# Mixer output of a hybrid decoder layer: four plain column blocks become two column pairs with partly Strassen products

## The chip, the cores and the metric

One core of one Trainium2 chip runs the whole layer in one launch. The metric is the device time of that launch in microseconds (us). TensorE is called PE, VectorE DVE, ScalarE ACT, GpSimd POOL; SP is the engine whose queue issues the weight loads. All data are float32.

## The reference

One decoder layer works on 256 tokens of width 2048. The part that matters here is the mixer's end and what follows it:

```
merged = sigmoid(gate_conv) * (y_conv @ Wa) + sigmoid(gate_hgrn) * (y_hgrn @ Wb)
x = layer_norm(ALPHA * x + merged @ mix_w_out[i], ln_g[i, 1], ln_b[i, 1])
x = layer_norm(ALPHA * x + 0.5 * swiglu(x, ffn2_w_in[i], ffn2_w_out[i]), ln_g[i, 2], ln_b[i, 2])
```

`merged` is 256 x 2048 and `mix_w_out` 2048 x 2048. The LayerNorm needs a whole row of 2048 before it can normalise any of it.

## The kernel before, in words

**Tiles.** The 256 tokens are two token tiles, t0 and t1. A k-tile is 128 rows of a weight; 2048 rows are sixteen k-tiles. A column block is 512 columns. One weight element is two k-tiles by 512 columns (128 x 1024 in SBUF, 512 KB). The tokens stand still in PE (transposed, 128 x 128) and the weight streams through.

**Three passes.** Each float32 factor is split into a high and a low part in the type fp32r: for a weight, ACT casts `raw` to `wh` (L1090) and DVE subtracts to get `wl` (L1101); for tokens, `halves` does the same (L299, L300). `passes` issues three matmuls of 512 columns per k-tile and token tile: L1160 (high, high), L1161 (`wl`), L1162 (token low). So a plain element that serves both token tiles costs PE 2 x 2 x 3 = 12 matmuls.

**The weight line.** `plan` lists all elements in the order of use. `feed` keeps the line going: a load by SP into `raw` (four buffers), a cast on ACT, a split on DVE, then PE. The pairs `wh`/`wl` come from a ring of six (`NMAIN`, called main); elements of a `Unit` may also take pairs of the stage's own ring, whose size stands in `EXTRA` ("merge": 2). A pair is free again when PE has used the element for both token tiles.

**Unit and Quad.** A `Unit` (`run_unit`) is one column block; it goes through blocks of elements, t0 first and then t1 within a block. A `Quad` (`run_quad`) is a pair of column blocks, where some k-tiles are done as Strassen products (in Winograd's form): k-tiles 0 to 7 are two steps of a 2 x 2 problem (tokens t0/t1, low and high k-tiles, left and right columns), and each step takes seven products instead of eight. A product is an element that serves one product alone: 6 matmuls on PE, one cast, one split. Four of the seven (`t1` to `t4`) need the sum of two weight buffers first, a DVE add (L1069). The eight weight buffers of a step sit in rings of their own, `raw11` (two buffers), `raw12`, `raw21`, `raw22` (one each), and a ring's next load waits until the buffer is done with. Names in `ORDER`: `11.0` is product 11 of step 0, `t3.1` is sum product 3 of step 1, `a0` and `u0` are plain elements for the left and the right block. Quad elements use the main ring only. The token operand needs four sums `s1` to `s4`, which DVE makes.

**The stages around the change.** In the stage "merge", `gate_units(c)` runs for c = 0 to 3: a Quad for the two gates, then two Units of 8 k-tiles for the two branches (L922 to L924). It leaves `merged` in the tiles `m`. When the last gate Quad is done, `to_stat` transposes `m` on PE and splits it into the operand `ms` (L904, L905, L910, L917).

Then come four Units, one for each column block of the mixer's output (L931 to L942). `epi_m` adds the result to `ALPHA * x` (L935) and takes the statistics (`ln_stat`, L425). The last block is cut into k-tiles 0 to 3 and then 4 to 15 (`LATE`): in that second part t0 runs through all of its twelve k-tiles before t1 starts. With t0's row complete, `layer_norm` runs for t0: `bn_aggr` (L448), the root (ACT, L434), four normalisations (L491); then, for each 512 columns, a transposition on PE (L286), scale and shift on ACT (L485) and the split (L299, L300) that makes the next stage's token operand `xh`/`xl`. The next stage is "lead2", the first column block of the second FFN.

All engines work their instructions off in the order in which Tile's scheduler has put them, which it does once, when the program is built.

Of the kernel before, what the change touches and what calls it, by code (L numbers as in the profile page):

```python
# [17 lines left out]
P = 128  # L18
D = 2048
S = 256  # L20
NT = 2
# [10 lines left out]
HIGH = {"11": 2, "12": 1, "21": 1, "22": 1}  # L32
EXTRA = {"lead1": 3, "ffn1": 0, "tail1": 4, "hgrn": 0, "merge": 2, "lead2": 3, "ffn2": 0, "tail2": 4, "ple": 1}
ALPHA = 2.0 ** 0.25
# [32 lines left out]
class Quad:  # L67
# [24 lines left out]
    }  # L92

    def __init__(self, stat, w, cols, width, after, form):
        self.stat, self.w, self.cols, self.width, self.after = stat, w, cols, width, after
        short = form == "short"
        self.shorted = not short
        order = self.ORDER[form].split()
        second = (("p3", 0), ("r", 1)) if form[:4] == "gate" else (("p3", "d"), ("p5", 1))
        made = {}  # L100
# [41 lines left out]
def hybrid_layer(ctx: ExitStack, tc: tile.TileContext, x, p, ln_g, ln_b, ffn1_w_in, ffn1_w_out, mix_w_in,  # L142
# [146 lines left out]
    def halves(stat, t, g, src, nb, tag, into=None):  # L289

        if into:
            h, l = into
        else:
            where, bufs = (region["pool"], 7) if tag == "s" else (op, 8)
# [5 lines left out]
        nc.vector.tensor_tensor(out=lf, in0=src, in1=hf.bitcast(F32), op=ALU.subtract)  # L300
        stat.parts[t, g] = (h, l)
# [120 lines left out]
    def ln_stat(t, c):  # L422
        if c == 0:
            stats[t] = st.tile([P, 4, 6], F32, tag="bn", name="bn", bufs=2)
        nc.vector.bn_stats(stats[t][:, c, :], xt[t][:, c * CC : (c + 1) * CC])  # L425
# [19 lines left out]
    def moments(t, scale):  # L445

        mv = st.tile([P, 2], F32, tag="mv", name="mv", bufs=2)
        nc.vector.bn_aggr(mv, stats[t])  # L448
        return mv[:, 0:1], rsqrt_of(mv[:, 1:2], 1, 1.0, LN_EPS / scale ** 2)
# [413 lines left out]
    def gate_units(c):  # L863
# [33 lines left out]
        def fifth(ps):  # L897
            both(made["conv", 1], made["conv", 1], ps["p4"], ALU.add)
            for key in (("conv", 1), ("hgrn", 0), ("hgrn", 1)):
                sigmoid(made[key])  # L900
            if c == 3:
                share_banks({"a": 4, "t": 4})
                load_stored()
                for i in range(4):  # L904
                    defer(2 + 3 * i, lambda t=i % 2, cc=i // 2: to_stat(ms, t, cc, mc[t, cc], 4, "x"))  # L905

# [5 lines left out]
        def epi_h(t, acc):  # L912
            m = mc[t, c] = made["conv", t] if c == 3 else rtile([P, CC], tag=f"m{t}{c}", name="m")
# [11 lines left out]

    mc = {}
    units.append(("merge", drain))
    for c in range(4):
        gate_units(c)

    for c in range(4):  # L931
        def epi_m(t, acc, c=c):
            settle(c)
            xc = xt[t][:, c * CC : (c + 1) * CC]
            nc.vector.scalar_tensor_tensor(out=xc, in0=xc, scalar=ALPHA, in1=acc, op0=ALU.mult, op1=ALU.add)  # L935
            ln_stat(t, c)
            if c == 3:
                layer_norm(t, 1, 1.0, x2)

        if c == 3:  # L940
            units.append(("merge", lambda: open_high("lead2")))
        units.append(Unit(ms, mix_w_out[0], 0, 16, c * CC, CC, epi_m, split=LATE if c == 3 else SPLIT))  # L942

# [238 lines left out]
    def run_quad(u, gi):  # L1182
        left = {}
        for el in u.els:
            for bank, _, ks in el["use"]:
                left[bank] = left.get(bank, 0) + len(ks)
        ps = {}
        for el in u.els:
            for i, (bank, t, ks) in enumerate(el["use"]):
                tick()  # L1190
                first = bank not in ps
                if first:
                    ps[bank] = ps["p1"] if bank == "r" else ptile("a", bank)
                for a, k in enumerate(ks):
                    left[bank] -= 1
                    passes(ps[bank], u.stat, t, k, gi, a if len(ks) > 1 else i, first and a == 0, left[bank] == 0)
            consumed(gi)
            while u.after and all(b in left and not left[b] for b in u.after[0][0]):
                _, fn, read = u.after.popleft()
                fn(ps)  # L1200
                for b in read:
                    used(ps[b])
            gi += 1
        return gi

# [44 lines left out]
```

## Time and profile before

| | |
|---|---|
| median of 3 runs | 2207.2 us (2206.49 to 2207.89) |
| the profiled execution | 2205.99 us, its span 2204.3 us |
| PE busy | 2183.2 us, 99% |
| DVE busy | 1805.5 us, 82% |
| ACT busy | 1171.4 us, 53% |
| gates and branches (stage "merge") | about 1060 to 1308 us |
| mixer's output, four Units | about 1308 to 1397 us |
| lead2 from | about 1397 us |

A time in a row of the timeline is counted from the start of the span. In the timeline a row gives start, duration, engine, line, operation and, in square brackets, how long the engine had been idle before it and who released it. A row with x3 is three instructions, merged. In a row of the windows each engine has its busy time and, in brackets, its number of instructions; PEclk is the granted clock of PE as a share.

### The profile page before, as it was taken

What the parts mean: (1) busy time and instruction counts of PE and PEld (TensorE: products, weight loads), DVE (VectorE), ACT (ScalarE), POOL (GpSimd) and SP (SyncE); (2) the same over time, 40 slices, a digit from 0 to 9 for tenths busy, and PEclk for the clock granted to TensorE, in tenths of its full rate; (3) what the DMA queues carried; (4) which work ended last, traced back from release to release, by engine and by line L of the source; (5) the groups of instructions that cost most, each with busy time, mean ns of one, the idle gap of its engine ahead of it and who ended that gap; (6) DMA issues with size and microseconds to landing.
All of it is one profiled execution on the core that took longest, in us unless ns stands there. A gap on an engine that the chain in (4) does not pass through costs nothing.

```text
span 2204.3 us, 27128 instructions
## 1 busy us (share of the span) xinstructions
PE 2183.2 (99%) x10043; PEld 1818.4 (82%) x10043; DVE 1805.5 (82%) x2046; ACT 1171.4 (53%) x1397; POOL 18.7 (1%) x48
## 2 busy tenths in 40 slices
PE   9999999999999999999999999999999999999997
PEld 7988888888887888888888888798888888888886
DVE  6799998999886677658898885679999999998667
ACT  5555555555565534534564553645555555555473
POOL 1000000000000000000000000000000000000000
PEclk9999999999999999999999999999999999999999
DMA  7666666666663665554666576466666666665564
GB/s 254 217 191 211 206 202 189 194 202 212 203 196 124 192 212 179 188 184 149 225 207 191 186 234 223 152 214 197 195 202 187 208 210 201 201 210 180 182 218 150
DMA packets 227129, 434.20 MB, mean 197 GB/s; under 512 B 14508, under 2 KB 23220, under 8 KB 226996
## 3 DMA queue, kind: packets, MB, share of 16 engines
q1 hardware_dynamic: 225716, 428.27, 61.3%
q0 software_dynamic: 1280, 4.20, 0.5%
q8 instruction: 78, 1.28, 0.2%
q14 instruction: 55, 0.45, 0.1%
HBM read 428.22 MB, written 4.19 MB: 196 GB/s over the span
## 4 chain that ended last, share of the span: by engine, by line
PE 92%; DVE 3%; DMA 2%; ACT 1%; issue 1%; DVEq 0%; SPq 0%; ACTq 0%
PE bank L1161 30%; PE bank L1162 30%; PE bank L1160 30%; DVE wl L1101 2%; PE bank L286 2%; PE bank L705 1%; DMA raw<-in_ffn_w_in_dram 1%; DMA raw<-in_ffn_w_out_dram 1%; ACT wh L1090 1%; DVE raw L1069 0%; DVE x L505 0%; DMA raw<-in_ple_w_gate_dram 0%; DVE x L506 0%; ACT y L485 0%; PE bank L675 0%
## 5 line engine op out<-in xcount | busy, mean ns | idle before, releaser
L1090 ACT CAST wh<-raw 128x1024 fp32r<-128x1024 f32 (+1 forms) x968 | 969.0, 1031 | 801.7 <-PE bank L1162 363.9
L1101 DVE TENSOR_TENSOR wl<-raw,wh 128x1024 fp32r<-128x1024 f32 (+1 forms) x968 | 1135.5, 1201 | 259.4 <-ACT wh L1090 246.4
L1162 PE MATMUL bank<-wh,xl 128*128 128x512 f32 (+1 forms) x1672 | 645.0, 387 | 2.6 <-DVE xl L300 2.5
L1161 PE MATMUL bank<-wl,xh 128*128 128x512 f32 (+1 forms) x1672 | 644.8, 387 | 0.3 <-DVE wl L1101 0.3
L1160 PE MATMUL bank<-wh,xh 128*128 128x512 f32 (+1 forms) x1672 | 636.7, 388 | 0.4 <-ACT wh L1090 0.2
L1162 PEld LDWEIGHTS bank<-wh,xl 128*128 128x128 f32 x1672 | 314.2, 188 | 65.0 <-DVE xl L300 5.2
L1160 PEld LDWEIGHTS bank<-wh,xh 128*128 128x128 f32 x1672 | 314.2, 188 | 60.9 <-ACT xh L299 0.7
L1161 PEld LDWEIGHTS bank<-wl,xh 128*128 128x128 f32 x1672 | 314.5, 188 | 60.0 <-DVE wl L1101 0.8
L1161 PE MATMUL bank<-wl,gh 128*128 128x512 f32 x896 | 349.2, 391 | 1.1 <-DVE wl L1101 1.1
L1162 PE MATMUL bank<-wh,gl 128*128 128x512 f32 x896 | 348.5, 390 | 0.0
L1160 PE MATMUL bank<-wh,gh 128*128 128x512 f32 x896 | 346.3, 393 | 0.1
L1069 DVE TENSOR_TENSOR raw<-raw,raw 128x1024 f32<-128x1024 f32 x208 | 245.5, 1181 | 13.6 <-DMA raw<-in_ffn_w_in_dram 7.2
L1161 PEld LDWEIGHTS bank<-wl,gh 128*128 128x128 f32 x896 | 168.3, 188 | 37.1 <-DVE wl L1101 3.1
L1160 PEld LDWEIGHTS bank<-wh,gh 128*128 128x128 f32 x896 | 168.2, 188 | 34.8 <-ACT gh L299 0.5
L1162 PEld LDWEIGHTS bank<-wh,gl 128*128 128x128 f32 x896 | 168.3, 188 | 34.7
L1161 PE MATMUL bank<-wl,sh 128*128 128x512 f32 x464 | 181.6, 391 | 0.0
L1162 PE MATMUL bank<-wh,sl 128*128 128x512 f32 x464 | 180.6, 389 | 0.0
L1160 PE MATMUL bank<-wh,sh 128*128 128x512 f32 x464 | 177.1, 389 | 0.0
L1160 PEld LDWEIGHTS bank<-wh,sh 128*128 128x128 f32 x464 | 87.1, 188 | 18.3
L1162 PEld LDWEIGHTS bank<-wh,sl 128*128 128x128 f32 x464 | 87.1, 188 | 17.8
L1161 PEld LDWEIGHTS bank<-wl,sh 128*128 128x128 f32 x464 | 87.1, 188 | 17.7
L299 ACT CAST gh<-bank 128x512 fp32r<-128x512 f32 (+2 forms) x54 | 30.6, 569 | 72.2 <-PE bank L286 71.6
(179 smaller groups left out, 1045.3 us busy)
## 6 DMA issues: line engine op xcount, KB each, us to landing
raw<-in_ffn_w_in_dram SPq DMA_DIRECT2D x288, 512.0 KB, 4.3
raw<-in_mix_w_in_dram SPq DMA_DIRECT2D x176, 512.0 KB, 4.6
raw<-in_ffn_w_out_dram SPq DMA_DIRECT2D x168, 512.0 KB, 4.8
raw<-in_ffn_w_in_dram SPq DMA_DIRECT2D x64, 256.0 KB, 3.0
raw<-in_mix_w_out_dram SPq DMA_DIRECT2D x32, 512.0 KB, 5.5
raw<-in_ple_w_gate_dram SPq DMA_DIRECT2D x32, 512.0 KB, 5.2
raw<-in_ffn_w_in_dram SPq DMA_DIRECT2D x32, 384.0 KB, 3.9
raw<-in_branch_w_conv_dram SPq DMA_DIRECT2D x16, 512.0 KB, 5.1
```

Source lines behind the costliest of these rows:

```text
L286: state["turned"] = nc.tensor.transpose(tp[:, i * P : (i + 1) * P], src[:, i * P : (i + 1) * P], ident).ins
L299: state["half"] = nc.scalar.copy(hf, src).ins
L705: nc.tensor.matmul(gp[:, (h * 2 + t) * 64 : (h * 2 + t + 1) * 64], kd[:, h, t * P : (t + 1) * P], qd[:, h, t, :], start=True, stop=True)
L1069: nc.vector.tensor_tensor(out=out, in0=a, in1=b, op=ALU.add)
L1090: nc.scalar.copy(h[:, :n, :w], raw[:, :n, :w])
L1101: state["split"] = nc.vector.tensor_tensor(out=l[:, :n, :w], in0=raw[:, :n, :w], in1=h[:, :n, :w].bitcast(F32), op=ALU.subtract).ins
L1160: nc.tensor.matmul(acc, sh, wh[:, a, :n], start=first, stop=False)
L1161: nc.tensor.matmul(acc, sh, wl[:, a, :n], start=False, stop=False)
L1162: nc.tensor.matmul(acc, sl, wh[:, a, :n], start=False, stop=last)
```

## The change

The four Units become two Quads, `mix_units(0)` and `mix_units(2)`, each with k-tiles 0 to 7 as Strassen products and 8 to 15 plain.

- A Quad has 14 products of 6 matmuls and 8 plain elements of 12: 180 matmuls for a pair, where two Units have 192. It has 22 elements (22 casts, 22 splits) where two Units have 16, and 8 weight adds.
- The token sums: `low_part` transposes `m` of the first two blocks soon after it is made, splits it (tag `m`), keeps a copy `mT`, and after the fourth makes the four sums; `fifth` of the last gate splits them.
- The results of the seven products are combined on DVE (`first`, `second`, `third`, `done`): twelve operations of 512 columns and four statistics for a pair, where two Units have four and four.
- The order of the last Quad, "mixend", has its last six plain elements in a tied group: `visit` runs all six for t0 and then all six for t1.
- The stage's own pairs `EXTRA["merge"]` go from 2 to 0.

```diff
+        "mix": "11.0 11.1 t1.0 a3 22.0 u3 t3.0 a0 t2.0 u0 21.0 t4.0 a1 t1.1 u1 22.1 t3.1 a2 t2.1 u2 21.1 t4.1",
+        "mixend": "11.0 11.1 t1.0 a3 22.0 t3.0 u3 t2.0 21.0 t4.0 t1.1 22.1 t3.1 t2.1 21.1 t4.1 [ a0 u0 a1 u1 a2 u2 ]",
...
-            if c == 3:
+            if c < 2:
+                defer(2, lambda: low_part(t, m))
+            elif c == 3:
                 defer(5 - t, lambda: to_stat(ms, t, 3, m, 4, "g"))
+        def low_part(t, m):
+            tp = transposed(m, 4)
+            halves(ms, t, c, tp, 4, "m")
+            mT[t, c] = rtile([P, CC], tag=f"mT{t}{c}", name="mT")
+            nc.scalar.copy(mT[t, c], tp)
+            if t + c == 2:
+                x11, x12, x21, x22 = mT[0, 0], mT[0, 1], mT[1, 0], mT[1, 1]
+                both(x22, x21, x22, ALU.subtract)
+                both(x21, x11, x21, ALU.subtract)
+                both(x11, x22, x11, ALU.subtract)
+                both(x12, x12, x11, ALU.add)
...
-        def epi_m(t, acc, c=c):
-            nc.vector.scalar_tensor_tensor(out=xc, in0=xc, scalar=ALPHA, in1=acc, op0=ALU.mult, op1=ALU.add)
-            ln_stat(t, c)
-            if c == 3:
-                layer_norm(t, 1, 1.0, x2)
-        units.append(Unit(ms, mix_w_out[0], 0, 16, c * CC, CC, epi_m, split=LATE if c == 3 else SPLIT))
+        def first(ps):
+            made["e"] = st.tile([P, CC], F32, tag="h", name="e", bufs=3)
+            nc.scalar.copy(made["e"], ps["p1"])
+            scaled(cols(0, 0), made["e"])
+        def second(ps):
+            for t in range(NT):
+                scaled(cols(t, 1), ps["p5"])
+        def third(ps):
+            e = made["e"]
+            both(e, e, ps["p6"], ALU.add)
+            both(cols(0, 1), cols(0, 1), e, ALU.subtract)
+            both(e, e, ps["p7"], ALU.add)
+            both(cols(1, 1), cols(1, 1), e, ALU.subtract)
+            scaled(cols(1, 0), e)
+        def done(t, n, bank):
+            def fn(ps):
+                both(cols(t, n), cols(t, n), ps[bank], ALU.add)
+                ln_stat(t, c + n)
+                if last and n:
+                    ...
+                    layer_norm(t, 1, 1.0, x2)
+    mix_units(0, False)
+    mix_units(2, True)
...
+        for group in u.groups:
+            for turn in range(2):
+                for n in group:
+                    if turn < len(u.els[n]["use"]):
+                        visit(u, n, turn, gi, ps, left)
```

The scheduler puts the instructions into their final order, so the order is shown at two places.

DVE before, in the middle of the mixer's output: four splits, then one result and its statistics for a column block (`wl` is a split, L935 the result, BN_STATS the statistics).

```order
L1101 TENSOR_TENSOR wl_10762<-raw_10689,wh_10761 128x1024
L1101 TENSOR_TENSOR wl_10775<-raw_10701,wh_10774 128x1024
L1101 TENSOR_TENSOR wl_10787<-raw_10713,wh_10786 128x1024
L1101 TENSOR_TENSOR wl_10799<-raw_10726,wh_10798 128x1024
L935 SCALAR_TENSOR_TENSOR x0_10359<-x0_10359,bank2_83 128x512
L425 BN_STATS bn_10677<-x0_10359 128x6
```

DVE now, where the first pair ends and the second begins: the first row is the split of `t4.1` of the first pair, the second that of `11.0` of the second pair; L1131 is a weight add, L957 a step that combines the first pair's results; `raw11_10831` is the weight buffer of the second pair's `11.1`.

```order
L1163 TENSOR_TENSOR wl_10828<-raw11_10300,wh_10827 128x1024
L1163 TENSOR_TENSOR wl_10840<-raw11_10682,wh_10839 128x1024
L1131 TENSOR_TENSOR raw11_10682<-raw11_10682,raw12_10753 128x1024
L957 TENSOR_TENSOR e_10613<-e_10613,bank6_87 128x512
L1131 TENSOR_TENSOR raw12_10753<-raw12_10753,raw22_10756 128x1024
L957 TENSOR_TENSOR x0_10397<-x0_10397,e_10613 128x512
L1163 TENSOR_TENSOR wl_10857<-raw11_10831,wh_10856 128x1024
L957 TENSOR_TENSOR e_10613<-e_10613,bank4_85 128x512
L1163 TENSOR_TENSOR wl_10867<-raw11_10682,wh_10866 128x1024
L957 TENSOR_TENSOR x0_10397<-x0_10397,bank2_83 128x512
L1163 TENSOR_TENSOR wl_10892<-raw_10695,wh_10891 128x1024
L957 TENSOR_TENSOR x0_10397<-x0_10397,bank7_88 128x512
```

Between two splits there now stand weight adds and the first pair's sums. From the split of `11.0` to the split of `t4.1` of the second pair, DVE has 15 splits, 8 adds and 18 operations of 512 columns in its order.

PE before, from t0's last matmul of the mixer's output (first row) to the first transposition of the normalised x (L286). Of the 24 matmuls between the two, all of them t1's (bank7), the first two and the last one are shown.

```order
L1162 MATMUL bank2_83<-wh_11021,gl_10567 128x512
L1160 MATMUL bank7_88<-wh_10935,xh_10485 128x512
L1161 MATMUL bank7_88<-wl_10936,xh_10485 128x512
...
L1162 MATMUL bank7_88<-wh_10997,gl_10508 128x512
L286 MATMUL bank4_85<-ident_89,x0_10359 128x128 x4
```

PE now, the same place: `wh_11127` is element `u2`, whose use with `gl_10583` in the third row is t0's last matmul; the fourth row is t1's (`gl_10632`), and L293 is the transposition.

```order
L1224 MATMUL bank4_85<-wh_11115,gl_10583 128x512
...
L1223 MATMUL bank3_84<-wl_11128,gh_10582 128x512
L1224 MATMUL bank3_84<-wh_11127,gl_10583 128x512
L1224 MATMUL bank1_82<-wh_11098,gl_10632 128x512
L293 MATMUL bank0_81<-ident_89,x0_10397 128x128 x4
L1222 MATMUL bank2_83<-wh_11115,gh_10631 128x512
L1223 MATMUL bank2_83<-wl_11116,gh_10631 128x512
```

The scheduler has put most of t1's matmuls of the tied group ahead of t0's last one: 1 of t1's matmuls is left between t0's last and the first transposition, and 12 more stand after that transposition. Before, it was 24 and 12. After those 12, both programs have the remaining transpositions and two matmuls of lead2 before the first one that reads `xl`.

More of the change, by code (lines that the diff above doesn't have):

```diff
@@ L97, in __init__ @@
         self.shorted = not short
-        order = self.ORDER[form].split()
-        second = (("p3", 0), ("r", 1)) if form[:4] == "gate" else (("p3", "d"), ("p5", 1))
+        text = self.ORDER[form]
+        order = text.replace("[", "").replace("]", "").split()
+        free, _, tied = text.partition("[")
+        n = len(free.split())
+        self.groups = [[i] for i in range(n)] + ([list(range(n, len(order)))] if tied else [])
+        second = (("p3", "d"), ("p5", 1)) if form in ("short", "long") else (("p3", 0), ("r", 1))
         made = {}
@@ L293, in halves @@
         else:
-            where, bufs = (region["pool"], 7) if tag == "s" else (op, 8)
+            where, bufs = {"s": (region["pool"], 7), "m": (region["pool"], 4)}.get(tag, (op, 8))
             h = where.tile([P, 4, P], F32R, tag=tag + "h", name=tag + "h", bufs=bufs)
@@ L1187, in run_quad, with visit @@
         ps = {}
[L1188 to L1204, printed above, removed]
+        for group in u.groups:
[3 more added lines that the diff above has]
+                        visit(u, n, turn, gi, ps, left)
+        return gi + len(u.els)
+    def visit(u, n, turn, gi, ps, left):
+        use = u.els[n]["use"]
+        bank, t, ks = use[turn]
+        tick()
+        first = bank not in ps
+        if first:
+            ps[bank] = ps["p1"] if bank == "r" else ptile("a", bank)
+        for a, k in enumerate(ks):
+            left[bank] -= 1
+            passes(ps[bank], u.stat, t, k, gi + n, a if len(ks) > 1 else turn, first and a == 0, left[bank] == 0)
+        if turn == len(use) - 1:
+            consumed(gi + n)
+        while u.after and all(b in left and not left[b] for b in u.after[0][0]):
+            _, fn, read = u.after.popleft()
+            fn(ps)
+            for b in read:
+                used(ps[b])
     gi = 0
```

40 lines of the change are left out of this document (27 added, 13 removed).

## The prediction

> **What bounds the kernel now.** The page first:
>
> ```profile
> PE 2183.2 (99%) x10043; PEld 1818.4 (82%) x10043; DVE 1805.5 (82%) x2046; ACT 1171.4 (53%) x1397; POOL 18.7 (1%) x48
> PE 92%; DVE 3%; DMA 2%; ACT 1%; issue 1%; DVEq 0%; SPq 0%; ACTq 0%
> ```
>
> The second line is the chain that ended last: PE bounds the kernel, so a matmul taken away is worth its full time as long as nothing else becomes late in that stage. DVE is next, with 82% on average. Its room differs by stage, so I read the windows: the last gate Quad first, then two stretches of the mixer's output (PE, PEld, DVE, ACT, POOL busy, clock, DMA share, GB/s).
>
> ```profile
> 1242.40:1283.30 40.90, 40.90 (x182) 33.78 (x181) 34.53 (x33) 23.01 (x25) 2.73 (x6) 1.00 0.48 148
> ```
>
> ```profile
> 1340.00:1360.00 20.00, 20.00 (x90) 16.57 (x89) 10.96 (x11) 7.10 (x7) 0.00 (x0) 1.00 0.65 210
> 1398.00:1400.05 2.05, 0.18 (x1) 0.00 (x0) 2.05 (x4) 0.83 (x1) 0.00 (x0) 1.00 0.97 347
> 1401.60:1405.00 3.40, 3.40 (x9) 2.31 (x8) 2.35 (x5) 3.40 (x8) 0.00 (x0) 0.50 0.81 259
> ```
>
> A gate Quad keeps DVE busy for 34.5 of 40.9 us with hardly anything but its weights (33 instructions, of which 30 are splits and adds); its sums fall due in the two branch Units behind it. The four plain Units use half of DVE. At the end of the mixer's output PE stands still for 1.9 us, and 1.5 us later its clock is halved for 3.4 us: the only such place in the kernel.
>
> The unit prices come from DVE's timeline: starts of neighbouring rows give what one instruction really takes from the queue.
>
> ```profile
> 1198.95 5.76 DVE L1101 TENSOR_TENSOR wl<-raw,wh 128x1024 fp32r<-128x1024 f32 x5
> 1204.63 1.22 DVE L1069 TENSOR_TENSOR raw<-raw,raw 128x1024 f32<-128x1024 f32 x1
> 1205.76 3.53 DVE L1101 TENSOR_TENSOR wl<-raw,wh 128x1024 fp32r<-128x1024 f32 x3
> ...
> 1301.34 0.68 DVE L867 TENSOR_TENSOR sig<-sig,bank 128x512 f32<-128x512 f32 x1
> 1301.94 1.22 DVE L1101 TENSOR_TENSOR wl<-raw,wh 128x1024 fp32r<-128x1024 f32 x1
> ...
> 1325.20 0.69 DVE L935 SCALAR_TENSOR_TENSOR x<-x,bank 128x512 f32<-128x512 f32 x1 [3.13 <-PE bank L1162]
> ...
> 1346.96 0.69 DVE L935 SCALAR_TENSOR_TENSOR x<-x,bank 128x512 f32<-128x512 f32 x1 [3.13 <-PE bank L1162]
> ```
>
> Five splits in 5.68 us and an add in 1.13: 1.14 us for either. An operation of 512 columns: 0.60. The last two rows are t0's results of two blocks, one Unit of 96 matmuls apart: 21.76 / 96 = 0.2267 us per matmul, so 2.72 us for a plain element and 1.36 for a product.
>
> **The change part by part.**
>
> *Matmuls.* 2 x 12 = 24 fewer: 24 x 0.2267 = **5.4 us** saved, if PE stays fed.
>
> *The gates.* Of `low_part`, the four transpositions and splits replace those of the first two blocks; new are four sums, four splits of them (8 x 0.60 = 4.8 us of DVE) and four copies on ACT. The stretch 1242 to 1283 has 6 us of DVE idle, each gate has another 21.8 us (96 matmuls) of branches behind it, and the additions spread over three gates: nothing, or up to 4.8 us if DVE were never idle there. The two missing spare pairs served branch Units alone, where PE takes 2.72 us per element and DVE 1.14: nothing.
>
> *The first pair.* DVE comes to it after the branches, with time to fill the six pairs. 30 x 1.14 + 16 x 0.60 = 43.8 us of DVE stand against 180 x 0.2267 = 40.8 us of PE, and its last sums slip into the second pair. No loss here.
>
> *The second pair.* It follows without a branch between, and starts with the first pair's sums in DVE's queue. How far can DVE be ahead? The six pairs set that, as ACT's row shows for a cast held up by PE, not by weights; and two rows give the landing time of a weight (median of this stage, then the spread before it).
>
> ```profile
> 1338.80 1.05 ACT L1090 CAST wh<-raw 128x1024 fp32r<-128x1024 f32 x1 [0.31 <-PE bank L1162]
> ```
>
> ```profile
> raw<-in_mix_w_out_dram SPq DMA_DIRECT2D x27, 512.0 KB, 5.5
> ```
>
> ```profile
> DMA to landing us min/median/max: 3.6/4.9/10.1
> ```
>
> `11.0` can be cast only when `t3.1`, six elements earlier, is used up; then PE still has `a2 t2.1 u2 21.1 t4.1`, 2 x 2.72 + 3 x 1.36 = 9.5 us. Less the cast (1.05) and the split (1.14), DVE's lead is 7.3 us at most. From there to the split of `t4.1` of this pair DVE has 15 splits, 8 adds and 18 small operations: 23 x 1.14 + 18 x 0.60 = 37.0 us. Besides, `11.1` needs the buffer that the split just ahead of `11.0`'s has freed: load 5.5 and cast 1.05, less 1.14 for the split between, makes 5.4 us, in which DVE has two adds and two sums (3.5): 1.9 us of waiting. Together 38.9 us. PE needs for the same 15 elements 13 x 1.36 + 2 x 2.72 = 23.1 us. PE idle: 38.9 - 7.3 - 23.1 = **8.5 us**. Behind it come six plain elements, where DVE gets ahead again, so nothing is added, but nothing is won back either. Ends: without the wait for the load and with a lead of 9.5 us, 4.4 us; with the longest landing, 10.1 us, 13.1. I take the median's value.
>
> *The end.* DVE's rows and PE's rows around the LayerNorm:
>
> ```profile
> 1387.76 0.69 DVE L935 SCALAR_TENSOR_TENSOR x<-x,bank 128x512 f32<-128x512 f32 x1 [7.21 <-PE bank L1162]
> ...
> 1392.37 1.92 DVE L491 TENSOR_SCALAR x<-x,mv,r 128x512 f32<-128x512 f32 x4
> 1394.20 4.63 DVE L1101 TENSOR_TENSOR wl<-raw,wh 128x1024 fp32r<-128x1024 f32 x4
> 1398.74 0.68 DVE L935 SCALAR_TENSOR_TENSOR x<-x,bank 128x512 f32<-128x512 f32 x1
> 1399.33 0.69 DVE L300 TENSOR_TENSOR xl<-yT,xh 128x512 fp32r<-128x512 f32 x1
> ```
>
> ```profile
> 1387.33 0.39 PE L1162 MATMUL bank<-wh,gl 128*128 128x512 f32 x1
> ...
> 1393.00 0.62 PE L286 MATMUL bank<-ident,x 128*128 128x128 f32 x4
> ...
> 1400.08 0.50 PE L1162 MATMUL bank<-wh,xl 128*128 128x512 f32 x1 [1.89 <-DVE xl L300]
> ```
>
> From t0's last matmul (1387.33) to the first transposition it is 5.7 us, filled before with 24 of t1's matmuls; from there to `xl`, another 7.1 us, with 12 more and the two of lead2. DVE's chain is the same now: sum, statistics, root, four normalisations, four splits, `xl`. But only 1 matmul of t1 is left for the first stretch. The 23 others have run earlier, ahead of t0's end, and hide nothing: 23 x 0.2267 = **5.2 us** of PE idle. Ends: 4.0, if a part of the chain is shorter because the left block's sum is done ahead of the right one's; 5.9, if that sum (0.60) is late as well.
>
> *Behind the restart.* t1 now has two sums and two statistics in DVE's queue ahead of the next `xl`, not one of each: 2 x 0.60 = **1.2 us**, since PE waits for these `xl`. The halved clock stays one period, as before. Ends: a loss of nothing, or of 1.2 and two more halved periods of 3.4 us, in each of which PE does half: 4.6.
>
> The trace has the clock halved after a stop of 1.9 us. The Trainium skill, TensorE: Matmul & The Clock Gate, section "Why this matters for your kernels", asks for no PE idle gaps above about 3 us between bursts of matmuls. The trace disagrees on the size: 1.89 us were enough here. By the page, the 5.2 us at the end alone would count, and the sum would stay as it is; by the trace, the stops within the second pair may count too, which is the third rival.
>
> *Sum.* - 5.4 + 8.5 + 5.2 + 1.2 = + 9.5 us. The profiled execution took 2205.99 us (span 2204.3 and 1.7 around it); it would take 2215.5. The median of the three runs lies 1.2 above it: **2216.7 us**.
>
> **The rivals.**
>
> *DVE keeps up.* If the lead is larger than I think or the sums fit into gaps, the second pair costs nothing: - 5.4 + 5.2 + 1.2 = + 1.0, 2208.2 us. For it speaks that in the last gate Quad DVE was busy for most of the time (34.5 of 40.9 us) and PE never stopped. Against it: that Quad had no sums of another one in its way. It decides at 38.9 us of DVE against 30.4 of lead and PE. Chance 0.16.
>
> *The cover is not needed.* As before, and DVE, now ahead, has t0's statistics almost done when t0 ends, so that the end costs what it cost before: - 5.4, 2201.8 us. This is the forecast's other side: faster. It decides at the 5.7 us between t0's last matmul and the transposition; those are a chain that starts with t0's last sum, which speaks against it. Chance 0.07.
>
> *The clock.* Each stop of 1.9 us or more is followed by a halved period, in the second pair and again after the restart: two periods more than before, 2 x 1.7 = 3.4 us: 2220.1 us. For it: the one case in the trace. Against it: PE waits for DVE in that stretch anyway, so a slow PE costs only what is left. Chance 0.15.
>
> **How the numbers follow.** The forecast has 0.62, the three rivals 0.16, 0.07 and 0.15. A measurement of this kernel can tell about 0.2% from no change, 4.4 us. The forecast's own ends, with the second pair at 4.4 and the end at 4.0, make - 5.4 + 4.4 + 4.0 + 0 = + 3.0 (2210.2); with the second pair at 11, between the median's and the longest landing, 5.9 and 1.2 make + 12.7 (2219.9), and with the clock's 3.4 it is 2223.3. I take 2207.5 to 2222: it holds the first rival and most of the third, and leaves out the second and the far ends. Faster by over 0.2% is the second rival alone, 0.07. Within 0.2% lie the first rival and the low end of the forecast, 0.16 + 0.05 = 0.21. Slower: 0.72.
>
> **What would show it.** Right: the timeline shows PE idle, released by the split (L1163), in the second half of the mixer's output, 6 to 11 us in all and most of it ahead of products of the second pair, with DVE at 95% and more from about the start of that pair; one stop of about 5 us right ahead of the transposition of x (L293), released by the normalisation; PE without stops in the gates. Wrong in its largest term: PE without waits for the split there; then the time lies near 2208. Wrong in the second: the transposition follows t0's last matmul with no stop. If PE stops in the gates, I have missed the cost of the earlier sums or of the missing pairs.

## The result, and the profile after

| | before | after |
|---|---|---|
| median of 4 runs | 2206.84 us (2206.26 to 2207.89) | 2221.72 us (2220.3 to 2223.46) |
| the profiled execution | 2205.99 us, span 2204.3 | 2223.46 us, span 2221.8 |

The ratio is 1.0068, with a 95% interval of 1.0056 to 1.008: slower by 14.9 us. The forecast was 2216.7 us, range 2207.5 to 2222.0. The direction held and the size was short by 5 us; the median lies just inside the range's upper end, by 0.3 us, and two of the four runs lie above it.

The page of after, the same two lines: 24 matmuls fewer, 52 instructions more on DVE and 22 more on ACT, and in the chain less PE, more of everything that PE waits for.

```profile
PE 2186.9 (98%) x10019; PEld 1816.2 (82%) x10019; DVE 1852.1 (83%) x2098; ACT 1189.7 (54%) x1419; POOL 18.6 (1%) x48
PE 90%; DVE 4%; DMA 3%; ACT 2%; issue 1%; DVEq 0%; SPq 0%; ACTq 0%
```

What PE waited for in after from 1340 to 1430 us (who waits, for whom, us in total, times, the longest). Before had one such row there, 1.9 us for `xl`.

```profile
PE bank L293 <- DVE x L498: 3.7, 1, 3.7
PE bank L1222 <- ACT wh L1152: 3.7, 5, 1.6
PE bank L1223 <- DVE wl L1163: 3.4, 2, 2.8
PE bank L1224 <- DVE xl L307: 1.8, 2, 1.3
PE bank L1222 <- ACT xh L306: 1.0, 1, 1.0
```

From the top: the stop at the LayerNorm; weights of the second pair, and one of lead2; splits of the second pair; token operands behind the restart (the last two). The casts in the second row are in the pair only the messenger: there each cast that PE waits for had itself waited for a DVE add.

The windows of after (PE, PEld, DVE, ACT, POOL, clock, DMA share, GB/s): the second pair, the LayerNorm, the restart, and what follows it.

```profile
1351.80:1385.90 34.10, 28.59 (x104) 20.77 (x103) 33.95 (x39) 15.60 (x17) 0.00 (x0) 0.90 0.25 77
1360.45:1367.25 6.80, 5.98 (x14) 4.72 (x15) 6.80 (x9) 1.12 (x2) 0.00 (x0) 0.50 0.75 231
1399.20:1403.30 4.10, 0.36 (x3) 0.03 (x1) 3.36 (x11) 2.53 (x3) 0.00 (x0) 1.00 0.00 0
1412.00:1419.00 7.00, 4.11 (x16) 2.45 (x14) 6.18 (x11) 6.74 (x13) 0.00 (x0) 0.96 0.80 245
1418.50:1425.20 6.70, 6.00 (x14) 4.75 (x15) 4.20 (x9) 2.55 (x4) 0.00 (x0) 0.50 0.69 231
```

In the pair DVE is busy for 33.95 of 34.10 us and PE for 28.6. The clock is halved twice for 6.8 us, in the pair and behind the restart; before it was once, for 3.4. (In both kernels it is halved once more at the very end, from 2193.5 us before and from 2213.8 after, where PE has no more work.)

To see where the time came from I set the same matmul of both executions side by side (counted from the start up to the end of the gates, and behind the pairs back from the end, so that the 24 missing ones drop out) and read how far after lags at six places, from the start of the stage "merge" on. The differences of neighbouring places are the cost of a stretch, in us, net of what before loses there; what the matmuls save is added back in the pairs.

| kernel | gates | pairs, to t0's end | t0's end to restart | restart to lead2's steady part | the rest |
|---|---|---|---|---|---|
| forecast | 0 | 8.5 | 5.2 | 1.2 | 0 |
| after | 1.1 | 10.9 | 3.3 | 6.6 | 1.2 |
| first pair only | 0.3 | 0.0 | -0.6 | 1.3 | 0.6 |
| second pair only | 0.3 | 2.1 | 4.2 | 0.1 | 0.0 |
| second pair only, t1 held | 0.3 | 4.6 | 0.0 | 1.8 | 0.8 |
| both, adds on POOL | 0.3 | 21.9 | 3.5 | -0.2 | 1.3 |
| both, t1 held | 0.3 | 11.8 | 0.0 | 1.4 | 1.7 |
| both, t1 held, first sums left out | 0.3 | 8.9 | 0.0 | 1.4 | 2.1 |
| both, t1 held, 11.1 late | 1.8 | 12.0 | 0.0 | 1.0 | 1.4 |
| both, t1 held, spread | 0.3 | 6.6 | 6.7 | 3.7 | 0.3 |
| both, t1 held, spread, casts behind | 0.3 | 5.2 | 2.8 | 4.7 | 1.5 |
| both, casts behind | 0.3 | 10.0 | 3.3 | 1.9 | 1.4 |
| first pair only, casts behind | 0.3 | 0.0 | -0.6 | 0.0 | 1.2 |
| first pair only, splits ahead | 0.3 | 0.0 | 4.7 | 3.8 | 0.7 |

The matmuls save 5.4 with both pairs and 2.7 with one. The table is of one profiled execution each, and ahead of the gates these differ from before by -0.8 to 1.5 us, which it leaves out; that of after is the slowest of its four, 1.7 us above their median. The ratios below are to the kernel before, run beside it on the same chip, and us from ratios are the ratio's excess times 2207.

**The second pair on DVE.** DVE's rows in after: the split of `11.0` is the last of the three in the first row (it ends at 1344.99), then come the split of `11.1` and that of `t4.1`. ACT's row holds the casts of the first pair's `t4.1` and of `11.0`, and PE's row is its first matmul of the second pair.

```profile
1341.35 3.64 DVE L1163 TENSOR_TENSOR wl<-raw,wh 128x1024 fp32r<-128x1024 f32 x3
...
1350.72 1.23 DVE L1163 TENSOR_TENSOR wl<-raw,wh 128x1024 fp32r<-128x1024 f32 x1 [2.13 <-ACT wh L1152]
...
1383.42 1.22 DVE L1163 TENSOR_TENSOR wl<-raw,wh 128x1024 fp32r<-128x1024 f32 x1
```

```profile
1341.55 2.00 ACT L1152 CAST wh<-raw 128x1024 fp32r<-128x1024 f32 x2 [2.11 <-DVE raw L1131]
```

```profile
1350.38 0.39 PE L1222 MATMUL bank<-wh,mh 128*128 128x512 f32 x1
```

From the end of the split of `11.0` to that of `t4.1` (1384.64) DVE took 39.6 us, and its lead over PE at the start, from the end of the split of `11.0` to its first use, was 1350.38 - 1344.99 = 5.4. With the prediction's 23.1 us of PE that makes 39.6 - 5.4 - 23.1 = 11.1 us lost; PE in fact took 10.9 us more for the 108 matmuls of the products, `a3` and `u3` than at full speed. The same sum fits the other kernels with both pairs: 9.8 against 9.6 with t1 held, 10.2 against 9.9 with the casts behind, 6.5 against 6.3 with the first sums left out, 9.8 against 9.5 with 11.1 late.

### The profile page after: what moved, and what is told of

The parts are those of the page before. It is cut to its first block, busy times and chain, and to the rows that moved or that the text cites. A ratio compares the mean times of both kernels' runs of the same rounds, so it can differ in the third digit from the quotient of the medians.

```text
span 2221.8 us, 27163 instructions
## 1 busy us (share of the span) xinstructions
PE 2186.9 (98%) x10019; PEld 1816.2 (82%) x10019; DVE 1852.1 (83%) x2098; ACT 1189.7 (54%) x1419; POOL 18.6 (1%) x48
## 3 DMA queue, kind: packets, MB, share of 16 engines
q8 instruction: 78, 1.28, 0.2%
## 4 chain that ended last, share of the span: by engine, by line
PE 90%; DVE 4%; DMA 3%; ACT 2%; issue 1%; DVEq 0%; SPq 0%; ACTq 0%
PE bank L1223 29%; PE bank L1222 29%; PE bank L1224 29%; DVE wl L1163 2%; PE bank L293 2%; DMA raw<-in_ffn_w_in_dram 1%; ACT wh L1152 1%; PE bank L712 1%; DMA raw<-in_mix_w_out_dram 1%; DVE raw L1131 0%; DMA raw<-in_branch_w_hgrn_dram 0%; DMA raw<-in_ple_w_gate_dram 0%; DVE x L512 0%; DVE x L513 0%; DVE bn L432 0%
## 5 line engine op out<-in xcount | busy, mean ns | idle before, releaser
L1152 ACT CAST wh<-raw 128x1024 fp32r<-128x1024 f32 (+1 forms) x980 | 981.7, 1031 | 781.3 <-PE bank L1224 329.2
L1163 DVE TENSOR_TENSOR wl<-raw,wh 128x1024 fp32r<-128x1024 f32 (+1 forms) x980 | 1149.0, 1201 | 235.7 <-ACT wh L1152 223.8
L1223 PE MATMUL bank<-wl,xh 128*128 128x512 f32 (+1 forms) x1640 | 634.3, 388 | 3.1 <-DVE wl L1163 3.1
L1224 PE MATMUL bank<-wh,xl 128*128 128x512 f32 (+1 forms) x1640 | 633.4, 387 | 2.5 <-DVE xl L307 2.4
L1222 PE MATMUL bank<-wh,xh 128*128 128x512 f32 (+1 forms) x1640 | 625.5, 389 | 3.6 <-ACT wh L1152 2.6
L1222 PEld LDWEIGHTS bank<-wh,xh 128*128 128x128 f32 x1640 | 309.0, 188 | 64.9 <-ACT wh L1152 4.3
L1224 PEld LDWEIGHTS bank<-wh,xl 128*128 128x128 f32 x1640 | 309.1, 188 | 63.7 <-DVE xl L307 4.9
L1223 PEld LDWEIGHTS bank<-wl,xh 128*128 128x128 f32 x1640 | 309.2, 189 | 62.2 <-DVE wl L1163 4.2
L1131 DVE TENSOR_TENSOR raw<-raw,raw 128x1024 f32<-128x1024 f32 x224 | 264.7, 1183 | 14.8 <-DMA raw<-in_ffn_w_in_dram 7.3
```

The source lines that it names most:

```text
L1131: nc.vector.tensor_tensor(out=out, in0=a, in1=b, op=ALU.add)
L1152: nc.scalar.copy(h[:, :n, :w], raw[:, :n, :w])
L1163: state["split"] = nc.vector.tensor_tensor(out=l[:, :n, :w], in0=raw[:, :n, :w], in1=h[:, :n, :w].bitcast(F32), op=ALU.subtract).ins
L1222: nc.tensor.matmul(acc, sh, wh[:, a, :n], start=first, stop=False)
L1223: nc.tensor.matmul(acc, sh, wl[:, a, :n], start=False, stop=False)
L1224: nc.tensor.matmul(acc, sl, wh[:, a, :n], start=False, stop=last)
```

## The experiments

**The two pairs apart.** In the first kernel the last two column blocks are plain Units with the old end, in the second the first two are.

```diff
     mix_units(0, False)
-    mix_units(2, True)
+    plain_unit(2)
+    plain_unit(3)
```

```diff
-    mix_units(0, False)
+    plain_unit(0)
+    plain_unit(1)
     mix_units(2, True)
```

> Only the first two column blocks are a Quad; the last two are plain Units with the old end (LATE). Theory (the loss sits in the second pair, in DVE's queue, and in what stands behind its end): the first pair has DVE's lead ahead of it and slack behind it, and the end is as it was. 12 matmuls fewer are -2.7 us, the gates keep the +1.1 that the trace of after shows there: 2205.2 us against 2206.8 before (2203.5 to 2207.5), no stop for the split L1163 in the mixer's output, one halved clock period. Rival 1 (a pair costs DVE more than it saves PE wherever it stands): half of the 10.9 us of the second pair comes back here: about 2210.

> The first two column blocks are plain Units, the last two the Quad with the tied end. Theory (the second pair starves because it follows the first): with plain elements ahead DVE reaches the pair with all six pairs full and none of the other pair's sums (10 operations, 6 us) in its queue: no stop for the split in the pair. Its end still lacks cover (in PE's order 8 of t1's matmuls stand between t0's last and the transposition, not 24): -2.7 +1.1 for the gates, +2 to 3.5 at the LayerNorm, +4 to 6.6 behind the restart with its clock: 2213 us (2210 to 2216). Rival 1 (the pair itself starves, whatever stands ahead): some 8 us more, 2220 or above. Rival 2 (the end costs nothing by itself, it only inherits the late weights): 2205 to 2207.

Measured: 2204.85 us, ratio 0.9988 (0.9979 to 0.9997), and 2210.5 us, 1.0013 (1.0004 to 1.0022). Each time lies in the theory's range, the second near its lower end. Not all terms came out: in the first kernel the clock was not halved in this part at all, and in the second the stretch behind the restart cost 0.1 us where 4 to 6.6 were expected. The windows of the two kernels, for the four blocks' stretch of the first and the pair of the second:

```profile
1300.00:1390.00 90.00, 90.00 (x404) 74.53 (x403) 73.01 (x80) 43.20 (x45) 0.00 (x0) 1.00 0.59 193
```

```profile
1345.00:1385.00 40.00, 38.72 (x169) 31.23 (x168) 37.30 (x38) 19.20 (x20) 0.00 (x0) 1.00 0.29 96
```

With the first pair alone PE never stops in 90 us. With the second alone it loses 1.3 of 40. The two ratios add up to +0.0001, 0.2 us; both pairs together are at +0.0068, 15 us. The first pair costs PE nothing by itself; the second, alone, is 2.9 us slower than before, most of it at its end. But the 15 us come only when the two stand back to back.

**The adds on POOL.**

```diff
+        engine = nc.gpsimd if el["src"][0].mix else nc.vector
-        nc.vector.tensor_tensor(out=out, in0=a, in1=b, op=ALU.add)
+        engine.tensor_tensor(out=out, in0=a, in1=b, op=ALU.add)
```

> Both pairs, but the 16 weight adds of the mixer's output run on POOL, which is idle there, in place of DVE. Theory (DVE's time is the cause in the second pair): 8 x 1.14 = 9.1 us of DVE's 38.9 go, 29.8 are left against 30.4 of lead and PE, so the stops in the second pair shrink to 0 to 3 us and the halved clock there goes: 8 to 11 us less than after, 2211 to 2214. The price of an add on POOL is in no trace here; if it takes 3 us or more, the products t1 to t4 wait for POOL instead, and the gain is less. Rival 1 (the wait for the buffer of 11.1 and the order of the ring cause the stops, not DVE's time): the stops stay, 2219 to 2223.

Measured: 2227.81 us, ratio 1.0092 (1.0078 to 1.0105): slower than after, and outside the theory's range and the rival's. The group of these adds in that kernel (x16, busy us, mean ns):

```profile
L1133 POOL TENSOR_TENSOR raw<-raw,raw 128x1024 f32<-128x1024 f32 x16 | 44.3, 2780 | 60.7 <-DMA raw<-in_mix_w_out_dram 34.9 <-DVE wl L1165 25.6
```

2.78 us each, where a split or add takes 1.14 of DVE's time, and they stand in one chain: `t1`, `t2` and `t4` of a step are all made in the same buffer, so each waits for the split of the one before (the last releaser in the row). The pairs cost 21.9 us in place of 10.9. The run says nothing against DVE's time as the cause; it only swaps it for a longer chain. The Trainium skill, GPSIMD Engine Reference, section "3.1 Elementwise — side-by-side cycle accounting", has an add of 2048 float32 columns about twice as slow there as on DVE. At 1024 columns the records give 2.78 us here against 1.22 on DVE, 2.3 times.

**t1 held behind t0.** The scheduler had pulled 23 of t1's matmuls ahead of t0's end. Here they wait for t0's last one.

```diff
+                end = state.get("mm")
                 for n in group:
                     if turn < len(u.els[n]["use"]):
-                        visit(u, n, turn, gi, ps, left)
+                        with tc.issue_after(end) if turn and len(group) > 1 else nullcontext():
+                            visit(u, n, turn, gi, ps, left)
```

> As after, but in the tied group t1's matmuls are held behind t0's last one on PE. 35 instead of 1 stand between t0's end and the transposition or just behind it. The last split that t0 needs ended at 1394.72 in after, and t0's last matmul started at 1398.92. Theory (the order of PE at the end costs): t0 ends about 2.5 us earlier, the transposition is covered and comes earlier by as much, and the next operands with it: 2.5 to 5 us less than after, 2217 to 2219. Rival 1 (t1's matmuls only filled time in which PE would have waited for weights): PE stops ahead of t0's end for what it saves behind it, 2221 to 2222.5.

> Only the second pair (2210.5 us above), with t1 held behind t0. Theory (of the second pair's loss without a pair ahead the most is the end's order, a stop of 3.6 us and a halved clock period of 6.8 us behind it): the stop goes, the halved period with it, and the usual stop of 1.5 to 2 us for xl comes back: 5 us less, 2205.5 us (2204 to 2207.5), the time of the run with the first pair alone. Rival 1 (PE waits for weights ahead of t0's end instead): 2208 to 2210.

Measured with both pairs: 2217.06 us, ratio 1.0036 (1.0022 to 1.005), 7 us less than after by the ratios, 4.7 by the medians, and at the theory's lower end. With the second pair alone: 2209.58 us, 1.0012 (1.0003 to 1.0021), against 1.0013 without the edit: nothing gained, the rival's case. The waits of PE in the two kernels with the second pair alone, first as it was, then with t1 held:

```profile
PE bank L293 <- DVE x L498: 3.5, 1, 3.5
PE bank L1238 <- ACT wh L1168: 1.3, 2, 0.8
...
```

```profile
PE bank L1240 <- DVE xl L307: 1.9, 1, 1.9
PE bank L1238 <- ACT wh L1168: 1.9, 4, 0.8
...
PE bank L1239 <- DVE wl L1179: 0.4, 1, 0.4
```

The stop at the LayerNorm goes and comes back as waits for weights ahead of t0's end and for `xl` behind the restart. In the table: 2.1 + 4.2 + 0.1 us against 4.6 + 0.0 + 1.8. With both pairs the first two stretches are 14.2 us without the edit and 11.8 with it; the larger part of its 7 us lies behind the restart, where 6.6 become 1.4.

**Less work for DVE.** On the kernel with t1 held, nine sums of the first pair are left out.

```diff
         def third(ps):
+            if not last:
+                return
...
-                both(cols(t, n), cols(t, n), ps[bank], ALU.add)
+                if last:
+                    both(cols(t, n), cols(t, n), ps[bank], ALU.add)
```

> As the run with t1 held behind t0 (2217.1 us), but of the first pair's results the nine sums that fall due from its products 6 and 7 on are left out (five in third, four in done), so its two column blocks come out incomplete; all weights, adds, splits and matmuls stay. Theory (DVE's queue is full from the start of the second pair, so all that it drops is won): 9 x 0.60 = 5.4 us less, 2211.5 us (2210 to 2213.5), and the stops for splits in the second pair shrink by as much. Rival 1 (the chain of one step's buffers, add, cast, split, add, sets the pace, DVE only looks full): 2216 to 2217.5.

Measured: 2210.2 us, ratio 1.002 (1.0011 to 1.0029); 3.5 us less than with the sums, where 5.4 were expected and the rival had at most 1. The intervals of the two ratios overlap, so it is the traces that decide: the pairs cost 8.9 us in place of 11.8. What DVE waited for from 1340 to 1395 us, with the sums and without them:

```profile
DVE wl L1163 <- ACT wh L1152: 3.0, 3, 1.7
...
```

```profile
DVE wl L1166 <- ACT wh L1155: 4.3, 3, 2.6
...
DVE raw L1134 <- DMA raw<-in_mix_w_out_dram: 0.4, 1, 0.4
```

Of the 5.4 us, 1.7 have turned into DVE's own waits for casts and loads, and about 3 are won: DVE's queue is the cause, with the next limit close behind it.

**11.1 later.**

```diff
-"mixend": "11.0 11.1 t1.0 a3 22.0 t3.0 u3 t2.0 21.0 t4.0 ...
+"mixend": "11.0 t1.0 a3 22.0 t3.0 t2.0 11.1 u3 21.0 t4.0 ...
```

> As the run with t1 held behind t0 (2217.1 us), but in the second pair product 11.1 comes behind t2.0, not straight behind 11.0, so that its buffer's load has time. Theory: DVE's wait for that cast (2.13 us in after, at 1352) goes, the rest of DVE's work is the same: 2 us less, 2215 us (2214 to 2216). Rival 1 (the wait is the larger part of the cause, and all stops hang on the late 11.1): 2210 to 2212. Rival 2 (t1.0 straight behind 11.0 makes a new wait, for the chain split, add, cast, split): 2217 to 2219.

Measured: 2214.29 us, ratio 1.0035 (1.0023 to 1.0048), against 1.0036 for its base. DVE's wait for that cast, 1.74 us in the base, is gone from the trace, and the pairs' stretch is 12.0 us against 11.8. Two us would be 0.0009, less than the intervals here, so the ratio can't decide. The trace shows why its stretch is no shorter: from the split of `11.0` to that of `t4.1` DVE took 37.2 us where the base took 39.3, so the wait is won, but its lead at the start was 4.3 in place of 6.3. Why DVE came later in this execution, which also lost 1.8 us in the gates, was not tried.

**The products spread out.** Two plain elements, `a0` and `u0`, are taken out of the tied group and put between the products; `11.1` comes late here too.

```diff
-"mixend": "11.0 11.1 t1.0 a3 22.0 t3.0 u3 t2.0 21.0 t4.0 t1.1 22.1 t3.1 t2.1 21.1 t4.1 [ a0 u0 a1 u1 a2 u2 ]"
+"mixend": "11.0 a3 t1.0 22.0 t3.0 a0 t2.0 11.1 u3 21.0 t4.0 u0 t1.1 22.1 t3.1 t2.1 21.1 t4.1 [ a1 u1 a2 u2 ]"
```

> As the run with t1 held behind t0 (2217.1 us), but the second pair's a0 and u0 are taken out of the tied group and put between the products, with 11.1 late; four plain elements stay tied. Theory (the second pair starves because 13 products stand ahead of its last six plain elements: per product DVE needs more than PE): by t4.1 DVE needs 41.2 less the 1.9 of the buffer, PE and the lead give 28.5 + 7.3: 3 to 4 us of stops in place of 8.5; 5 us less, 2212 us (2210 to 2214). The end keeps 24 matmuls of cover up to the transposition, but none behind it up to the next operand: up to 2.7 us of that may come back. Rival 1 (the six pairs or the load of the buffers hold DVE back, not its work): 2216 or above.

Measured: 2220.5 us, ratio 1.0064 (1.0051 to 1.0076): worse than its base by 6 us, although the pairs' stretch did shrink by 5 (11.8 to 6.6). The same 40 us of both kernels, first the base, then the spread one:

```profile
1345.00:1385.00 40.00, 33.78 (x136) 26.13 (x135) 38.12 (x43) 17.34 (x19) 0.00 (x0) 0.96 0.26 86
```

```profile
1345.00:1385.00 40.00, 36.60 (x154) 28.14 (x153) 39.95 (x45) 18.84 (x20) 0.00 (x0) 1.00 0.32 110
```

DVE is now busy throughout and PE is busy for 2.8 us more. But the end takes it back. ACT in the spread kernel, around the root (start, duration, operation, idle time before it and the releaser), and DVE's row that needs the root:

```profile
1392.53 1.05 ACT L1152 CAST wh<-raw 128x1024 fp32r<-128x1024 f32 x1 [1.73 <-DMA raw<-in_ffn_w_in_dram]
1394.32 1.05 ACT L1152 CAST wh<-raw 128x1024 fp32r<-128x1024 f32 x1 [0.75 <-DMA raw<-in_ffn_w_in_dram]
1396.50 1.05 ACT L1152 CAST wh<-raw 128x1024 fp32r<-128x1024 f32 x1 [1.13 <-PE bank L1224]
1397.56 1.28 ACT L441 ACT_TABLE_LOAD   x1
1398.86 0.20 ACT L441 ACTIVATE r<-w 128x1 f32<-128x1 f32 x1
```

```profile
1399.09 0.16 DVE L443 RECIPROCAL r<-r 128x1 f32<-128x1 f32 x1 [4.10 <-ACT r L441]
```

The statistics were ready at 1394.9. The root stands behind casts of lead2's weights, which wait for loads and for a free pair, and behind a table load of 1.28 us: DVE waits 4.1 us for a root of 0.2.

**The casts behind the tokens.** The same is seen in after, behind the restart. ACT there: `xh` is the token cast, the rows between are weight casts of lead2.

```profile
1406.03 1.50 ACT L492 ACTIVATE yT<-bank,gbT 128x128 f32<-128x128 f32 x4
1409.34 1.05 ACT L1152 CAST wh<-raw 128x1024 fp32r<-128x1024 f32 x1 [1.81 <-DMA raw<-in_ffn_w_in_dram]
1410.30 0.62 ACT L306 CAST xh<-yT 128x512 fp32r<-128x512 f32 x1
```

The token operand is ready for its cast at 1407.5 and gets it at 1410.3. So in after, in the spread kernel and in the one with the first pair alone, the fifth to eighth of these casts are put behind the third token cast in ACT's order (for after as below; in the spread one, those from lead2's second weight on also wait for the root).

```diff
             halves(stat, t, c, y, 4, "x")
+            if i == 1 and t == 0 and c == 2:
+                gate["hi"] = state["half"], 4
+                state["hold"] = None
+                feed()
+        if i == 1 and t == 0:
+            state["hold"] = cur["cast"] + 4
...
-        nc.scalar.copy(h[:, :n, :w], raw[:, :n, :w])
+        with gated("hi"):
+            nc.scalar.copy(h[:, :n, :w], raw[:, :n, :w])
...
-        if i == len(plan) or i > cur["split"] + 1:
+        if i == len(plan) or i > cur["split"] + 1 or i == state.get("hold"):
```

> As after, but on ACT the fifth to eighth weight casts of lead2, which in after stand among the scalings and casts of the tokens and wait there for their loads (1.81 us ahead of the cast at 1409.34, 0.64 ahead of the next), are put behind the third token cast xh. Theory (what stands behind the restart is ACT's queue: a cast that waits for its load holds up xh, and with it DVE's xl and PE): the stops of 0.65, 1.15 and 1.78 us go but for up to 1.5 us at the fifth weight, whose split then comes at about 1414.8, and the double halved period behind them with them: 2 to 5.5 us less than after, 2216 to 2219.5. Rival 1 (the loads of lead2 come late in any case, the fifth weight stops PE for as long): 2221 to 2223.

> As the run with a0 and u0 spread among the products (2220.5 us), but on ACT lead2's weight casts from its second on stand behind the root, and the fifth to eighth behind the third xh. In the spread run the stops of the pair had shrunk as expected, but DVE waited 4.10 us for the root, which stood behind three casts that waited for loads and for a free pair, and PE stood for 2.6 us and later 2.9. Theory (ACT's queue gives back what spreading wins): the root comes some 3 us earlier, the stop ahead of the transposition goes to 0 to 0.5, one or two halved periods of 3.4 us with it: 2213 to 2217 us. Rival 1 (with four tied elements the end is too short in any case): 2219 to 2222.

> As the run with the first pair alone (2204.9 us), with the fifth to eighth weight casts of lead2 behind the third xh on ACT. Behind its restart there is one stop of 0.9 us. Theory: that stop shrinks, 0 to 0.9 us less, 2204 to 2205. Rival 1 (the held casts come too late for PE): 2206 or above.

Measured: 2216.62 us, ratio 1.0042 (1.003 to 1.0055), for both pairs, 5.7 us less than after; 2215.7 us, 1.0036 (1.0023 to 1.0048), for the spread one, 6 less than without the edit; 2203.78 us, 0.9984 (0.9975 to 0.9993), for the first pair alone, against 0.9988, which the intervals don't tell apart. The first two lie in the theory's range, the third 0.2 us below it. PE's waits in the first of the three (the rows of the transpositions and `xl` behind the restart are what to look for):

```profile
PE bank L1229 <- ACT wh L1159: 4.6, 6, 1.6
PE bank L293 <- DVE x L504: 3.7, 1, 3.7
PE bank L1230 <- DVE wl L1170: 3.1, 2, 2.6
PE bank L293 <- ACT yT L492: 1.2, 1, 1.2
```

The waits for `xl` and `xh` are gone, the 3.7 us at the LayerNorm are untouched, and one wait for a weight of lead2 (1.6) is left, as expected. In the table only the stretch behind the restart moves much, 6.6 to 1.9. Of these 4.7 us about 1.5 are shorter stops (3.1 us in after from the wait of 0.49 on, 1.6 now); up to 3.4 are the double halved period, which did not come there.

**Splits ahead of the normalisation.** One more run has a text on record that was written for another kernel (the one before, without its two spare pairs) and that breaks off before its numbers:

> As before, but without the stage's two spare weight pairs (EXTRA merge 0 in place of 2); no Strassen in the mixer's output. PLACEHOLDER

What ran under it is the kernel with the first pair alone, in which lead2's first two splits no longer have to stand behind the second normalisation. So nothing was predicted for this run, and the price of the two spare pairs by themselves was not tried.

```diff
-            if c == 1 and t == 0:
+            if c == 1 and t == 0 and i != 1:
                 gate["lo"] = norm.ins, 2
```

Measured: 2210.0 us, ratio 1.0013 (1.0003 to 1.0022), against 0.9988 with the old rule: 5.5 us more. DVE there:

```profile
1389.42 0.16 DVE L443 RECIPROCAL r<-r 128x1 f32<-128x1 f32 x1 [0.29 <-ACT r L441]
1390.36 1.22 DVE L1179 TENSOR_TENSOR wl<-raw,wh 128x1024 fp32r<-128x1024 f32 x1 [0.77 <-ACT wh L1168]
1391.50 0.21 DVE L445 SCALAR_TENSOR_TENSOR u<-r,m 128x1 f32<-128x1 f32 x1
```

It is the same trap on another engine: a split that waits for its cast stands ahead of the next step of the root, and PE stands for 3.7 us at the transposition.

## Why the prediction was right in direction and short in size

**The matmuls**, -5.4 us: as worked out. The page counts 10043 and 10019.

**The gates**, 0: right. The profiled execution of after has 1.1 us there, but of the twelve other kernels with the same gates eleven are at 0.3 in the table, and one at 1.8.

**The first pair**, 0: right. Alone it costs 0.0 us in the table.

**The second pair**, 8.5 us: the mechanism is the one described, and 10.9 us the size. The two kernels with one pair each show that it needs both; leaving out the first pair's sums shows that DVE's queue carries it. The term that was mis-sized is the lead: 7.3 us in the sum, 5.4 measured. The prediction let the six pairs set it. But the cast of `11.0` stood behind that of the first pair's `t4.1`, which had waited 2.11 us for an add on DVE: DVE's own queue was the limit before the six pairs were. The first pair needs 43.8 us of DVE against 40.8 of PE; that costs PE nothing there, but it eats the lead. In the other kernels with both pairs that are listed above the lead was 3.0 to 6.7 us, never 7.3. DVE's own chain was 39.6 us in place of 38.9, with a wait for the buffer of `11.1` of 2.13 in place of 1.9. The sum's 8.5 us were called PE idle; in fact PE stood for 5.4 us, below the 6 to 11 named as a sign, and lost the rest by running slowly, partly at half clock (6.8 us of the stretch), partly with wider spacing behind its stops (from 1384.34 on 0.35 us from one matmul to the next in place of 0.23).

**The half clock in the second pair** cost nothing net. From the start of the split of `11.1` on, DVE worked without a pause of its own, and from there to the end of PE's products it took 35.0 us in after, with 6.8 us at half clock, and 35.0 us both with t1 held and with the casts behind, with 3.4 us at half clock. A slower PE only waited less for DVE.

**The end**, 5.2 us: one stop of 3.7 us, right where it was said to be; the whole stretch cost 3.3, net of before's. It is smaller than 5.2 because the root came 0.53 us after DVE was ready for it, in place of 1.99 before. But the reason given, that t1's 23 matmuls have run too early, holds only in part: held back with the second pair alone, they won nothing. They had filled time in which PE would have waited for weights. The cover was not lost by the order; it was used up by the late weights.

**Behind the restart**, 1.2 us: this step failed, by 5.4 us. I counted DVE's two extra sums and statistics and took ACT as free, since the page has it at 54%. In fact `xh` stood behind weight casts that waited for their loads, and PE behind `xh`; moving the casts took the stretch from 6.6 to 1.9. A halved clock is part of the 6.6, about 1.7 net of before's. That is not the whole account. Seven kernels whose casts were not moved lie between -0.2 and 1.8 there, among them the one with both pairs and t1 held, at 1.4, where a cast also waits 1.83 us for its load ahead of an `xh`. What spares them was not tried, nor was holding t1 and moving the casts together. (The two spread ones, with four tied elements only, are at 3.7 and 4.7, and the one with the splits ahead at 3.8; what else is late in the spread ones was not tried.)

**The rivals.** DVE keeping up and a cover that isn't needed are refuted for both pairs together. The clock's rival named the places rightly: after has three halved periods more than before, where the rival had two. But its price did not come as it said: the two in the second pair cost nothing net, as the prediction had argued, and only the extra one behind the restart is left, up to 1.7 us. That its 2220.1 us lie nearer to the measured time than the forecast is luck. So is, in part, the forecast's own nearness: the end was too dear by 1.9 us where the second pair was too cheap by 2.4 and the restart by 5.4.

## What to carry to other kernels

Fewer matmuls pay where the engine that prepares operands has slack at that place and behind it: one Strassen pair with plain work on both sides gained 2.6 us, and 3.5 with the casts moved, the fastest version here; two in a row lost 15. In a queue that works in order, an instruction that waits for a load must not stand ahead of a short step on which another engine waits: three kernels lost 5 to 6 us to casts or splits in such a place, though in others the same order cost little. A lead that spare buffers allow is an upper bound; the queue that fills them may give less, here 5.4 us in place of 7.3. And before counting lost cover as a loss, ask whether the work that moved would otherwise have waited.

## What the runs showed of the hardware

**The clock is halved by the idle share of a fixed piece of time, not by the length of a stop.** Counted from the first row of the clock's records, all changes fall on multiples of 3.413 us. In each of the fourteen profiled kernels I took PE's idle time in each such piece between 1050 and 1440 us at full clock: all 15 pieces with 1.89 us or more were followed by a halved one, of the 8 with 1.69 to 1.87 five were, and none with 1.65 or less. Three pieces of after, in windows:

```profile
1357.03:1360.44 3.41, 1.45 (x7) 0.87 (x5) 3.41 (x5) 0.86 (x1) 0.00 (x0) 1.00 0.36 132
...
1397.99:1401.40 3.41, 1.54 (x7) 0.94 (x5) 3.05 (x7) 2.53 (x3) 0.00 (x0) 1.00 0.09 32
1401.40:1404.81 3.41, 1.54 (x9) 1.36 (x10) 2.77 (x10) 1.42 (x5) 0.00 (x0) 1.00 0.00 0
```

The first, 1.96 us idle, is followed by the halved piece at 1360.44. The other two share the longest stop of the kernel, 3.74 us at the LayerNorm, as 1.87 and 1.87, and neither is followed by one. So where a stop falls on the grid decides. That the same kernel may therefore lose it or not from run to run is not shown, with one profiled execution of each. Once halved, the limit is lower: of 29 such pieces the nine with 0.69 us of idle or more were followed by another, the twenty with 0.57 or less by full clock. The Trainium skill, TensorE: Matmul & The Clock Gate, section "What's actually happening", gives a free-running window of 3413 ns, which agrees, and one idle window as the condition; the pieces here were a bit more than half idle.
